# Moving one head pair's projection and convolution out of the delta stage into the seven-product stream, by way of DRAM

## The chip, the cores and the metric

One core of one Trainium2 chip runs the whole layer. The metric is the device time of one execution in microseconds (us). PE is TensorE, DVE is VectorE, ACT is ScalarE, POOL is GpSimd, SP is SyncE, whose queue issues most DMAs here.

## The reference, cut to what matters

The input is 1024 prompt rows and 64 rows of a running stream, 1088 rows of width 1024 in all. Branch B, the part that the change touches, has eight heads of 128; two heads make a *pair*, p = 0 to 3.

```python
y = einsum("bsd,de->bse", x, w_in)            # one projection, split into q, k, v, gates, ...
u = causal_conv(y[q|k|v of B], state_conv)    # width 4 along the rows, per channel, then SiLU
q, k = l2norm(q), l2norm(k)
per chunk of 64 rows:                         # 17 chunks: 16 of the prompt, 1 of the stream
    M     = strict_lower(beta * k k^T * decay)
    T     = inverse(I + M)
    v_new = T (beta v) - T (beta k decay) S   # S: state of the chunk before, 128x128 per head
    o     = q S decay + (q k^T * decay) v_new
    S     = S * decay + k^T v_new
Y_B = W_oB(rmsnorm(o) * silu(z_B))
x  <- LayerNorm(ALPHA * x + W_out(sig(g_A) * Y_A + sig(g_B) * Y_B))   # Y_A: window attention
```

## The kernel before, in words

Every fp32 product is made of three matmuls on rounded halves (hi·hi, hi·lo, lo·hi). The 1088 rows lie in SBUF as eight tiles `ring`, and weights come as tiles of 128 output channels (`wraw`, split into `whi`, `wlo`).

A weight tile is applied in one of two ways. **Direct** (`project`): three row groups of 384, 384 and 320 columns, 24 matmuls each, 72 matmuls and 26,112 columns for a tile. **Seven-product** (`stream`): two weight tiles together as a 2x2 block product with seven multiplications on quarter rows of 272 columns, 168 matmuls for both tiles; it needs sums of the input rows in SBUF (`ring2`), which are there only until attention ends.

The program runs in this order, in us of the profiled execution: loading, keys and values of branch A (0 to 117); `front`, a run of wide seven-product jobs for branch A's queries and its gate z (to 243); attention woven with narrow seven-product jobs of the merge gates (to 490); then branch B's delta stage (to about 1200), the two output projections, `out_b` and `final`.

The delta stage weaves two programs. The *chain* goes pair by pair: `ahead` (`logs`, `decay`, `products`, then `blocks`, a serial solve of 16x16 blocks on DVE), `steps` (17 delta steps, with `prep` a group of chunks ahead), `norm`. The *fill* is independent projection work: `pair_project` of the next pair (six tiles: q, k, v of two heads, each followed by the convolution on ACT and DVE into `plb`), a merge gate, `zb_project` of the pair before (two tiles), and at the end `out_a`. Each `yield` of the chain asks for so many fill columns before PE goes on with the chain: `PROD` behind each group of products, `BLOCKS[p]` behind the solve, the three of `STEP` behind the three parts of a step, `SHORT` in `prep` and `norm`. PE keeps this program order. The other engines are ordered by a scheduler: urgent work first, then chain, then fill. The chain of pair 0 can start when four of its six tiles are projected (`READY`).

The names in the rows: `pj` and `bg` are PSUM banks; `pre` and `acc` the convolution's input and running sum (L812: three taps for each row group, after a first tap on ACT); `gt` a gate or tanh buffer; L819 writes SiLU into `plb`; L833 the same for z_B. In `blocks`, `nF` (L891) comes just before the solve, L915 and L917 are its 15 rounds, `XC` (L921) its result; `prep` starts with `X` on POOL (L938) and PE's `X,MT`. In a step, `S,plb` is the product with the state, `R` L999, `R,U` the solve's product, `vn` L1009, `vn,t2k` the state update's product, `S` L1024.

Of the kernel before, what the change touches and what calls it, by code (L numbers as in the profile page):

```python
# [11 lines left out]
F32 = mybir.dt.float32  # L12
F32R = mybir.dt.float32r
# [9 lines left out]
SEQ = 1024  # L23
# [22 lines left out]
NORM = 11984  # L46
STEP = (2200, 2100, 1450)
PROD = 3672
# [7 lines left out]
class Build:  # L56
# [477 lines left out]
    def load_rope(self, pool, name):  # L534
        cs = self.t(pool, [128, 2, NT], "cs")
        self.nc.sync.dma_start(cs, self.I[name])
        self.cosT, self.sinT = cs[:, 0], cs[:, 1]
# [49 lines left out]
    def front(self):  # L587
# [3 lines left out]
        def query(j):  # L591
            held = {}

            def ev(m, a, ps, add):
                g, h = divmod(a // HN, 2)
                first = (m, g) not in held
                if first:
                    held[m, g] = self.t(self.rq, [128, 2, 2 * HN], "qsp", F32R, bufs=4)
                q = held[m, g]
# [18 lines left out]
            return ev  # L618

        def gate(dst, t, silu):  # L620
            def ev(m, a, ps, add):
                src = ps
                if add is not None:
                    src = self.t(self.gsp, [128, HN], "gs", bufs=5)
                    self.land(src, ps, add)
                th = self.t(self.gsp, [128, HN], "gs", bufs=5)
                with self.urgent():
                    nc.scalar.activation(th, src, AF.Tanh, scale=0.5)
                    if silu:
                        nc.vector.scalar_tensor_tensor(th, th, 1.0, src, ALU.add, ALU.mult)  # L630
                nc.sync.dma_start(dst[t + m, :, a : a + HN], th)
            return ev

        def jobs():
            yield True, query(0)
            yield True, gate(self.zA, 2, True)
            for j in range(1, 4):
                yield True, query(j)
            yield True, gate(self.zA, 4, True)
            yield True, gate(self.zA, 6, True)  # L640
            self.done = True
            for i in range(0, 16 - sum(GATES), 2):
                yield False, gate((self.gA, self.gB)[i // 8], i % 8, False)
# [137 lines left out]


    def pair_project(self, p, qkv):
        nc = self.nc
        self.order = LATER if p == 0 else EARLY
        for s in range(3):
            for h in range(2):
# [35 lines left out]

                yield from self.project(ev, edge=p + s + h == 0, w=None if p + s + h else self.first)
                self.ready[p] += 1

    def zb_project(self, p):
        nc = self.nc
        for h in range(2):
            def ev(g, a, n, ps):  # L830
                th = self.t(self.mp, [128, 384], "gt", bufs=4)
                nc.scalar.activation(th[:, :n], ps, AF.Tanh, scale=0.5)
                nc.vector.scalar_tensor_tensor(th[:, :n], th[:, :n], 1.0, ps, ALU.add, ALU.mult)  # L833
                nc.sync.dma_start(self.zsd[2 * p + h, :, a : a + n], th[:, :n])
            last = p == NPAIR - 1
            yield from self.project(ev, edge=last and h == 1, soon=last)

# [404 lines left out]
    def fills(self, qkv):  # L1242
# [3 lines left out]
        for p in range(NPAIR + 1):  # L1246
# [5 lines left out]
            if p > 0:  # L1252
                yield from self.gate_project([next(gates) for _ in range(GATES[p - 1])])
                yield from self.zb_project(p - 1)
            if p < NPAIR:
                yield from self.pair_project(p, qkv[p])
# [7 lines left out]
    def run(self):  # L1264
        tc = self.tc
        with ExitStack() as es:
# [10 lines left out]
            self.k_d = dp.tile([2, 64, 4, KW], F32, tag="k_d", name="k_d")  # L1277
            self.qd = dp.tile([2, 512, 2 * NT], F32, tag="q_d", name="q_d")
            self.hp = tc.cur_priority
            tc.cur_priority = self.hp + 1_000_000  # L1280
# [17 lines left out]
            with tc.tile_pool(name="mp", bufs=1) as self.mp:  # L1298
                with tc.tile_pool(name="plb", bufs=2) as self.plb:
                    with tc.tile_pool(name="bp", bufs=1) as self.bp:  # L1300
                        qkv, D = {}, [{} for _ in range(NPAIR)]
                        fill = self.fills(qkv)
                        next(fill)
                        before = iter(())
# [144 lines left out]
```

## Time and profile before

| | |
|---|---|
| three runs | 1408.94, 1410.66, 1410.67 us, median 1410.66 |
| the profiled execution | 1408.06 us, span 1406.3 us |
| busy | PE 97%, DVE 70%, ACT 44%, POOL 16% of the span |
| granted PE clock | 0.995 of full speed in the mean |
| DMA | 162.47 MB in 152,500 packets, 116 GB/s in the mean |

PE is busy nearly the whole span, so the time is the columns that PE streams plus the few places where it waits. How busy another engine is in the mean says little: it matters where PE waits for it.

### The profile page before, as it was taken

The numbers are of one execution on the slowest core, as the hardware profiler recorded it, in microseconds if no ns is written. First come the engines' busy times: TensorE is split into PE (matmuls) and PEld (weight loads), VectorE is DVE, ScalarE is ACT, GpSimd is POOL, SyncE is SP. The second block draws the span as 40 slices with busy tenths as digits, with TensorE's granted clock in tenths as the row PEclk, the third lists the DMA queues.
The fourth block names the chain that finished last, engine by engine and source line by source line (L and its number), as shares of the span: only waits on it lengthen the run. The fifth ranks groups of instructions, "written<-read, shape, count | busy, mean of one in ns | idle before, by whom it ended". The sixth has DMA issues, their size and how long they took to land. (4 is left out here: it accounts for less than half of the span.)

```text
span 1406.3 us, 30878 instructions
## 1 busy us (share of the span) xinstructions
PE 1364.9 (97%) x11850; PEld 1270.8 (90%) x11850; DVE 989.3 (70%) x2404; ACT 624.0 (44%) x1764; POOL 231.8 (16%) x379
## 2 busy tenths in 40 slices
PE   8889999999999999999999999999998999999997
PEld 7889999999989899988999889988998889999886
DVE  8668555877777568867796777867788555655675
ACT  5263444555555444356633665256642443422000
POOL 4323223111111023111221113021220100000000
PEclk9999999999999999999999999999999999999998
DMA  7425566666665420210321003210346225564221
GB/s 241 117 79 131 144 135 183 190 183 180 170 183 165 123 87 31 73 36 17 93 80 57 32 24 100 82 57 17 124 137 226 73 74 167 192 219 137 95 94 71
DMA packets 152500, 162.47 MB, mean 116 GB/s; under 512 B 54304, under 2 KB 135840, under 8 KB 151968
## 3 DMA queue, kind: packets, MB, share of 16 engines
q1 hardware_dynamic: 138368, 148.59, 35.4%
q10 hardware_dynamic: 13632, 10.78, 2.5%
q8 instruction: 94, 1.54, 0.5%
q0 software_dynamic: 352, 1.11, 0.2%
q14 instruction: 54, 0.44, 0.1%
HBM read 111.74 MB, written 48.70 MB: 114 GB/s over the span
## 5 line engine op out<-in xcount | busy, mean ns | idle before, releaser
L108 PE MATMUL pj<-ring,whi 128*128 128x384 f32 (+2 forms) x2856 | 678.3, 327 | 5.8 <-DVE gt L1134 4.0
L108 PEld LDWEIGHTS pj<-ring,whi 128*128 128x128 f32 x2856 | 480.1, 189 | 17.2 <-issue 13.3
L108 PE MATMUL pj<-ring,wlo 128*128 128x384 f32 (+2 forms) x1680 | 466.2, 321 | 0.9 <-DVE rsh L471 0.8
L108 PEld LDWEIGHTS pj<-ring,wlo 128*128 128x128 f32 x1680 | 288.4, 188 | 5.8 <-issue 4.1
L812 DVE SCALAR_TENSOR_TENSOR acc<-pre,sm,acc 128x384 f32<-128x384 f32 (+1 forms) x216 | 134.0, 627 | 24.2 <-ACT acc L810 20.7
L108 PE MATMUL pj<-ring,wx 128*128 128x272 f32 x756 | 109.7, 291 | 2.9 <-ACT u L365 2.8
L88 ACT ACTIVATE whi<-wraw 128x1024 fp32r<-128x1024 f32 (+2 forms) x72 | 66.7, 927 | 82.4 <-PE pj L108 48.8
L108 PEld LDWEIGHTS pj<-ring,wx 128*128 128x128 f32 x756 | 99.6, 188 | 3.8 <-ACT u L365 3.8
L91 DVE TENSOR_TENSOR wlo<-wraw,whi 128x1024 fp32r<-128x1024 f32 (+2 forms) x58 | 68.0, 1172 | 40.4 <-ACT whi L88 35.3
L108 PE MATMUL bg<-ring,whi 128*128 128x384 f32 (+2 forms) x408 | 84.5, 317 | 5.6 <-ACT ring L88 5.2
L108 PEld LDWEIGHTS bg<-ring,whi 128*128 128x128 f32 x408 | 65.6, 190 | 7.0 <-ACT ring L88 5.2
L108 PE MATMUL pj<-pl,ring 128*128 128x512 f32 (+1 forms) x240 | 70.1, 375 | 0.0
L704 ACT ACTIVATE P<-bg,nm 128x192 f32<-128x192 f32 (+2 forms) x136 | 54.4, 408 | 33.4 <-DVE nm L697 32.1
L1024 DVE SCALAR_TENSOR_TENSOR S<-S,dec,bg 128x128 f32<-128x128 f32 x128 | 38.7, 344 | 39.2 <-PE bg L108 38.3
L813 ACT ACTIVATE gt<-acc 128x384 f32<-128x384 f32 (+1 forms) x72 | 36.4, 505 | 62.3 <-DVE acc L812 62.0
L108 PE MATMUL bg<-ring,wlo 128*128 128x272 f32 (+2 forms) x288 | 63.5, 307 | 0.0
L1002 ACT ACTIVATE qs<-bg,egs 64x128 f32<-64x128 f32 x128 | 46.4, 362 | 29.1 <-DVE R L999 27.4
L999 DVE SCALAR_TENSOR_TENSOR R<-bg,negc,t2k 64x128 f32<-64x128 f32 x128 | 44.6, 348 | 16.1 <-PE bg L108 14.9
L336 POOL TENSOR_TENSOR sums<-wraw 128x512 f32<-128x512 f32 x14 | 18.3, 1308 | 220.4 <-DMA wraw<-w_tiles 109.4
L819 DVE SCALAR_TENSOR_TENSOR plb<-gt,acc 128x384 f32<-128x384 f32 (+1 forms) x96 | 43.1, 461 | 15.6 <-ACT gt L813 15.3
L108 PEld LDWEIGHTS pj<-pl,ring 128*128 128x128 f32 x240 | 44.1, 188 | 8.2
L810 ACT ACTIVATE acc<-pre,sm 128x384 f32<-128x384 f32 (+1 forms) x72 | 42.8, 597 | 15.6 <-DVE plb L819 5.9
(277 smaller groups left out, 2317.3 us busy)
## 6 DMA issues: line engine op xcount, KB each, us to landing
wraw<-w_tiles SPq DMA_DIRECT2D x80, 512.0 KB, 3.9
q_d<-qsp SPq DMA_DIRECT2D x32, 256.0 KB, 3.5
keys<-k_d SPq DMA_DIRECT2D x28, 256.0 KB, 4.2
q<-q_d SPq DMA_DIRECT2D x64, 96.0 KB, 2.7
gA_d<-gs SPq DMA_DIRECT2D x32, 136.0 KB, 2.2
plb<-prodA SPq DMA_DIRECT2D x8, 544.0 KB, 4.4
plb<-prodB SPq DMA_DIRECT2D x8, 544.0 KB, 5.1
z<-zA_d SPq DMA_DIRECT2D x16, 256.0 KB, 3.2
```

What stands on the lines that cost most here:

```text
L88: i = self.nc.scalar.activation(hi, raw, AF.Copy)
L91: self.nc.vector.tensor_tensor(lo, raw, hi.bitcast(F32), ALU.subtract)
L108: self.tc.keep_in_program_order(self.nc.tensor.matmul(o, l, r, start=start, stop=stop, skip_group_check=skip))
L336: sub = lambda d, x, y, op: nc.gpsimd.tensor_tensor(d, x, y, op)
L704: nc.scalar.activation(P[:, hf, k], ps[:, k], AF.Exp, bias=nm[:, hf, b : b + 1], scale=0.125, accum_out=sm[:, hf, b : b + 1])
L810: nc.scalar.activation(acc[:, :w], pre[:, 0:w], AF.Copy, scale=cw(0))
L812: nc.vector.scalar_tensor_tensor(acc[:, :w], pre[:, j : j + w], cw(j), acc[:, :w], ALU.mult, ALU.add)
L813: nc.scalar.activation(th[:, :w], acc[:, :w], AF.Tanh, scale=0.5)
L819: nc.vector.scalar_tensor_tensor(o, v(th), 1.0, v(acc), ALU.add, ALU.mult)
L999: nc.vector.scalar_tensor_tensor(R[HS[h]], ks[HS[h], col[h]], self.negc[HS[h], p, c : c + 1], e["vs"][HS[h], i], ALU.mult, ALU.add)
L1002: nc.scalar.activation(qs[HS[1 - h]], ks[HS[1 - h], col[h]], AF.Copy, scale=self.egs[HS[1 - h], p, c : c + 1])
L1024: nc.vector.scalar_tensor_tensor(Sn[:, h], S[:, h], self.egl[h][:, p, c : c + 1], kv[:, 0:128], ALU.mult, ALU.add)
```

## The change

The six tiles of pair 0 leave the delta stage's fill. They become three wide seven-product jobs `conv(0..2)` (q, k, v; both heads at once) in `front`, between the last query job and the last two z jobs. A job's evacuations land in one tile of whole rows (1024 prompt rows, three state columns, 64 stream rows). When all four quarters of a head are there, the convolution runs once over 1091 columns instead of three times over 384, 384 and 323, and the result goes to DRAM (`conv_d`). After attention, `pair_load` brings it into `plb` with six DMAs in runs of 64 elements, k and q at once, v later, and POOL makes the second copy of k.

Pair 0's z_B tiles, which were fill, are drained before the chain starts (144 matmuls), and `STEP` falls from (2200, 2100, 1450) to (1300, 1500, 1350). `BLOCKS`, `PROD`, `SHORT`, `NORM` stay.

```diff
-STEP = (2200, 2100, 1450)
+STEP = (1300, 1500, 1350)
...
+        def conv(s):
+            held, left, acc = {}, [4, 4], []
+
+            def ev(m, a, ps, add):
+                if m not in held:
+                    held[m] = self.t(self.rq, [128, 4 * HN + 8], "qsp", bufs=4)
+                pre = held[m]
+                n = min(HN, SEQ - a)
+                for d, c in ((3 + a, slice(0, n)), (1030, slice(n, HN)))[: 1 + (n < HN)]:
+                    c0, w = c.start, c.stop - c.start
+                    self.land(pre[:, d : d + w], ps[:, c], None if add is None else add[:, c])
+                left[m] -= 1
+                if left[m]:
+                    return
+                if not acc:
+                    acc.append(self.t(self.rq, [128, 2, NT + 4], "cs"))
+                ct, w = 8 * s + m, NT + 3
+                x, y = acc[0][:, m, :w], pre[:, :w]
+                nc.gpsimd.memset(pre[:, 0:3], 0.0)
+                nc.gpsimd.tensor_copy(pre[:, 1027:1030], self.sconv[:, ct, :])
+                nc.gpsimd.tensor_copy(self.ncv[:, ct, 0, :], pre[:, 1024:1027])
+                nc.gpsimd.tensor_copy(self.ncv[:, ct, 1, :], pre[:, 1091:1094])
+                cw = lambda j: self.convw[:, ct, j : j + 1]
+                nc.scalar.activation(x, y, AF.Copy, scale=cw(0))
+                for j in range(1, 4):
+                    nc.vector.scalar_tensor_tensor(x, pre[:, j : j + w], cw(j), x, ALU.mult, ALU.add)
+                nc.scalar.activation(y, x, AF.Tanh, scale=0.5)
+                nc.vector.scalar_tensor_tensor(y, y, 1.0, x, ALU.add, ALU.mult)
+                nc.sync.dma_start(self.conv_d[2 * s + m, :, :SEQ], pre[:, :SEQ])
+                nc.sync.dma_start(self.conv_d[2 * s + m, :, SEQ:], pre[:, 1027 : 1027 + DEC])
+            return ev
...
+            for s in range(3):
+                yield True, conv(s)
...
+    def pair_load(self, qkv):
+        nc = self.nc
+        rows = lambda s, h: self.conv_d[2 * s + h].rearrange("p (c t) -> p c t", t=CH)
+        with self.urgent():
+            for h in range(2):
+                nc.sync.dma_start(qkv[0][:, :, 4 + h], rows(1, h))
+                nc.sync.dma_start(qkv[0][:, :, 1 + h], rows(0, h))
+        for h in range(2):
+            nc.gpsimd.tensor_copy(qkv[0][:, :, 3 * h], qkv[0][:, :, 4 + h])
+        for h in range(2):
+            nc.sync.dma_start(qkv[1][:, :, h], rows(2, h))
+        self.ready[0] = 6
...
-        self.order = LATER if p == 0 else EARLY
...
-                yield from self.project(ev, edge=p + s + h == 0, w=None if p + s + h else self.first)
+                yield from self.project(ev)
...
-            last = p == NPAIR - 1
-            yield from self.project(ev, edge=last and h == 1, soon=last)
+            first, last = p + h == 0, p == NPAIR - 1
+            self.order = LATER if p == 0 else EARLY
+            yield from self.project(ev, edge=first or last and h == 1, w=self.first if first else None, soon=last)
...
+            if p == 0:
+                self.pair_load(qkv[0])
+            elif p < NPAIR:
                 yield from self.pair_project(p, qkv[p])
...
-                        next(fill)
+                        for _ in range(2 * 72):
+                            next(fill)
```

On **DVE**, inside pair 0's block solve (the rounds L915 and L917, in the changed program L964 and L966), before:

```order
L917 TENSOR_REDUCE t2k_7550<-t2k_7554 128x2x5
L915 TENSOR_TENSOR t2k_7554<-t2k_7550,t2k_7548 128x2x6x6
L819 SCALAR_TENSOR_TENSOR plb_6816<-gt_7720,acc_7719 128x4x64
L917 TENSOR_REDUCE t2k_7550<-t2k_7554 128x2x6
L819 SCALAR_TENSOR_TENSOR plb_6816<-gt_7720,acc_7719 128x64
L915 TENSOR_TENSOR t2k_7554<-t2k_7550,t2k_7548 128x2x7x7
L833 SCALAR_TENSOR_TENSOR gt_7760<-gt_7760,pj_7735 128x384
L917 TENSOR_REDUCE t2k_7550<-t2k_7554 128x2x7
```

and after, at the same rounds:

```order
L860 SCALAR_TENSOR_TENSOR acc_8233<-pre_8230,sm_220,acc_8233 128x384
L964 TENSOR_TENSOR t2k_8024<-t2k_8020,t2k_8018 128x2x8x8
L860 SCALAR_TENSOR_TENSOR acc_8233<-pre_8230,sm_220,acc_8233 128x384
L966 TENSOR_REDUCE t2k_8020<-t2k_8024 128x2x8
L860 SCALAR_TENSOR_TENSOR acc_8233<-pre_8230,sm_220,acc_8233 128x384
L964 TENSOR_TENSOR t2k_8024<-t2k_8020,t2k_8018 128x2x9x9
L966 TENSOR_REDUCE t2k_8020<-t2k_8024 128x2x9
L867 SCALAR_TENSOR_TENSOR plb_7585<-gt_8234,acc_8233 128x6x64
```

Convolution taps of pair 1 stand between the rounds where the end of pair 0's convolution and z_B work stood. Counted over the whole order (DVE instructions of the fill between the marks, before to after):

| pair | last product to `nF` | `nF` to `XC` | `XC` to the first `R` |
|---|---|---|---|
| 0 | 4 acc, 1 plb, 1 wlo: the same | acc 9 to 19, plb 6 to 9, gt 3 to 0 | acc 0 to 8, plb 1 to 4, gt 3 to 0 |
| 1 | 5 acc, 4 plb to 1 gt, 1 wlo | acc 0 to 19, plb 0 to 6, gt 2 to 0 | acc 6 to 11, plb 2 to 8, gt 4 to 0 |
| 2 | 1 acc, 3 plb to 1 gt | acc 0 to 9, plb 0 to 2, gt 4 to 2 | acc 0 to 6, plb 1 to 5, gt 2 to 0 |
| 3 | 5 acc, 4 plb, 2 gt to 1 plb | the same | gt 1 to 3, wlo 0 to 1 |

In the steps themselves, from the first to the last `R` of a pair, the order holds 30, 28, 30 and 0 acc before, and 18, 21, 22 and 0 after.

On **PE**, one delta step, before (`S,plb` opens the step, `R,U` follows `R`, `vn` rows close it; `pj` rows are fill):

```order
L108 MATMUL bg_8197<-S_8178,plb_6816 128x128 x2
L108 MATMUL bg_8206<-X_8040,MT_7309 32x32 x8
L108 MATMUL pj_8167<-ring_107,whi_8003 128x384
L108 MATMUL pj_8167<-ring_107,wlo_8004 128x384
L108 MATMUL pj_8167<-ring_108,whi_8003 128x384 x2
L108 MATMUL pj_8167<-ring_108,wlo_8004 128x384
L108 MATMUL pj_8167<-ring_109,whi_8003 128x384
L108 MATMUL bg_8225<-R_8200,U_7884 128x128
```

and after:

```order
L108 MATMUL bg_8720<-S_8689,plb_7576 128x128 x2
L108 MATMUL bg_8729<-X_8569,MT_7768 32x32 x8
L108 MATMUL pj_8716<-ring_106,whi_8533 128x384 x2
L108 MATMUL pj_8716<-ring_106,wlo_8534 128x384
L108 MATMUL bg_8745<-R_8723,U_8391 128x128
```

Of six fill matmuls between the state's product and `R,U` three are left here. In the mean over the steps the fill between them falls from 2091 to 1299 columns, between `R,U` and the `vn` products from 2221 to 1509, and between those and the next step from 1440 to 1339.

On **SP's queue**, after attention, the changed program issues this, where before only weight tiles and gate stores stood:

```order
L146 DMA wraw_7673<-w_tiles 128x1024
L823 DMA plb_7576<-conv_d 128x17x64
L824 DMA plb_7576<-conv_d 128x17x64
L823 DMA plb_7576<-conv_d 128x17x64
L824 DMA plb_7576<-conv_d 128x17x64
L882 DMA zs_d<-gt_7661 128x384
L882 DMA zs_d<-gt_7665 128x384
L882 DMA zs_d<-gt_7669 128x320
L146 DMA wraw_7777<-w_tiles 128x1024
```

Four loads of k and q stand ahead of the stores of z_B and of the next weight tile; the two of v stand a few rows later.

## Rows read from the trace of the kernel before

**Rows 1.** The page: the span, and each engine's busy time and instructions.

```profile
span 1406.3 us, 30878 instructions
PE 1364.9 (97%) x11850; PEld 1270.8 (90%) x11850; DVE 989.3 (70%) x2404; ACT 624.0 (44%) x1764; POOL 231.8 (16%) x379
```

**Rows 2.** Busy time by stretch: `front`, direct projection, pair 0's first `prep`, pair 0's steps.

```profile
core 0: us, PE busy (x) PEld busy (x) DVE busy (x) ACT busy (x) POOL busy (x), PEclk, DMA share, GB/s
165.00:240.00 75.00, 75.00 (x600) 75.00 (x599) 40.27 (x76) 32.80 (x74) 18.79 (x14) 1.00 0.72 175
505.00:540.00 35.00, 35.00 (x214) 35.00 (x213) 27.83 (x49) 19.41 (x41) 6.18 (x20) 1.00 0.14 46
593.00:604.00 11.00, 10.78 (x220) 9.35 (x221) 6.23 (x15) 4.58 (x16) 3.57 (x5) 1.00 0.30 100
604.00:683.00 79.00, 78.69 (x963) 68.64 (x962) 59.71 (x162) 49.19 (x160) 11.67 (x33) 1.00 0.09 27
```

**Rows 3.** PE's waits, whole span: total us, times, longest us.

```profile
PE bg L108 <- ACT vn L1009: 2.1, 6, 0.6
PE bg L108 <- POOL X L938: 1.7, 3, 0.7
PE bg L108 <- DVE R L999: 0.4, 1, 0.4
```

**Rows 4.** Busy time from `nF` to `XC`, pairs 0 to 3 (columns of rows 2).

```profile
565.20:592.40 27.20, 27.20 (x168) 27.17 (x167) 25.36 (x59) 9.06 (x18) 2.92 (x8) 1.00 0.18 60
726.20:747.50 21.30, 21.30 (x132) 21.30 (x131) 19.96 (x44) 5.76 (x10) 0.00 (x0) 1.00 0.20 70
888.70:911.30 22.60, 22.60 (x139) 22.54 (x138) 20.68 (x45) 5.87 (x10) 0.00 (x0) 1.00 0.26 89
1049.20:1084.60 35.40, 31.43 (x179) 30.96 (x177) 33.40 (x59) 14.35 (x17) 0.00 (x0) 0.95 0.67 222
```

**Rows 5.** PE's timeline at the first `X,MT` of pairs 0, 1 and 2.

```profile
593.22 0.45 PE L108 MATMUL bg<-X,MT 32*32 32x32 f32 x32 [0.47 <-POOL X L938]
...
758.05 0.45 PE L108 MATMUL bg<-X,MT 32*32 32x32 f32 x32
...
912.11 0.45 PE L108 MATMUL bg<-X,MT 32*32 32x32 f32 x32 [0.57 <-POOL X L938]
```

**Rows 6.** The page's costly groups and DVE's by form: busy us, mean ns | idle.

```profile
L812 DVE SCALAR_TENSOR_TENSOR acc<-pre,sm,acc 128x384 f32<-128x384 f32 (+1 forms) x216 | 134.0, 627 | 24.2 <-ACT acc L810 20.7
L819 DVE SCALAR_TENSOR_TENSOR plb<-gt,acc 128x384 f32<-128x384 f32 (+1 forms) x96 | 43.1, 461 | 15.6 <-ACT gt L813 15.3
L833 DVE SCALAR_TENSOR_TENSOR gt<-gt,pj 128x384 f32<-128x384 f32 (+1 forms) x21 | 10.8, 520 | 1.2 <-ACT gt L832 1.1
L91 DVE TENSOR_TENSOR qsp<-rraw,qsp 128x272 fp32r<-128x272 f32 x26 | 14.6, 561 | 6.9 <-ACT qsp L88 6.9
L91 DVE TENSOR_TENSOR wlo<-wraw,whi 128x1024 fp32r<-128x1024 f32 x52 | 64.9, 1249 | 36.5 <-ACT whi L88 31.5 <-PE bg L108 4.8
L893 DVE TENSOR_TENSOR MT<-MT,nF 128x1088 f32<-128x1088 f32 x4 | 5.2, 1291 | 0.1
```

**Rows 7.** One delta step of pair 0 in the timeline.

```profile
645.50 0.61 PE L108 MATMUL bg<-S,plb 128*128 128x128 f32 x4
...
646.49 0.71 DVE L999 SCALAR_TENSOR_TENSOR R<-bg,negc,t2k 64x128 f32<-64x128 f32 x2
648.09 0.38 PE L108 MATMUL bg<-R,U 128*128 128x128 f32 x2
648.51 0.37 ACT L1009 ACTIVATE vn<-bg,F 128x128 f32<-128x128 f32 x1 [0.48 <-PE bg L108]
649.46 0.45 PE L108 MATMUL bg<-vn,t2k 64*64 64x128 f32 x8
```

**Rows 8.** The page's DMA issues: KB each, median us to landing.

```profile
q_d<-qsp SPq DMA_DIRECT2D x32, 256.0 KB, 3.5
plb<-prodA SPq DMA_DIRECT2D x8, 544.0 KB, 4.4
```

More of the change, by code (lines that the diff above doesn't have):

```diff
@@ L534, in load_rope @@
     def load_rope(self, pool, name):
-        cs = self.t(pool, [128, 2, NT], "cs")
+        cs = self.t(pool, [128, 2, NT + 4], "cs")[:, :, :NT]
         self.nc.sync.dma_start(cs, self.I[name])
@@ L597, in ev @@
                 if first:
-                    held[m, g] = self.t(self.rq, [128, 2, 2 * HN], "qsp", F32R, bufs=4)
+                    held[m, g] = self.t(self.rq, [128, 4 * HN + 8], "qsp", F32R, bufs=4)[:, : 4 * HN].rearrange("p (s n) -> p s n", s=2)
                 q = held[m, g]
@@ L1254, in fills @@
                 yield from self.zb_project(p - 1)
-            if p < NPAIR:
+            if p == 0:
+                self.pair_load(qkv[0])
+            elif p < NPAIR:
                 yield from self.pair_project(p, qkv[p])
@@ L1278, in run @@
             self.qd = dp.tile([2, 512, 2 * NT], F32, tag="q_d", name="q_d")
+            self.conv_d = dp.tile([6, 128, NT], F32, tag="conv_d", name="conv_d")
             self.hp = tc.cur_priority
@@ L1396 @@
     qp = query_pairs()
-    cols = kc + zc[0:2] + qp[0] + zc[2:4] + qp[1] + qp[2] + qp[3] + zc[4:8]
+    conv = lambda p: [2560 + 1024 * s + 128 * (2 * p + h) + ar for s in range(3) for h in range(2)]
+    cols = kc + zc[0:2] + qp[0] + zc[2:4] + qp[1] + qp[2] + qp[3] + conv(0) + zc[4:8]
     gates = iter([6672 + 128 * t + ar for t in range(16)])
@@ L1400 @@
     for p in range(NPAIR):
-        for s in range(3):
-            cols += [2560 + 1024 * s + 128 * (2 * p + h) + ar for h in range(2)]
+        cols += conv(p) if p else []
         cols += [next(gates) for _ in range(GATES[p])]
```

## Prediction

> **What bounds the kernel now.** I read the page first: PE is busy 1364.9 of 1406.3 us [rows 1], and DVE, the next engine, 989.3. So the time is PE's columns plus PE's waits, and a change is worth the columns that it saves less the waits that it opens. Then I read two stretches for the price of a column [rows 2]. In `front`, PE runs 600 matmuls of 272 columns in 75.00 us, 0.125 us each; in the direct projection it runs 214 in 35.00 us, 0.1636 us each, at 26,112 / 72 = 363 columns, so 0.451 us for 1000 columns. Both are without a gap at full clock.
>
> Third, the waits. In the whole span the delta stage's own links make PE wait very little: 2.1 us for `vn`, 1.7 us for `X` behind the block solves, 0.4 us for `R` [rows 3]. But look at how near those waits are. Between `nF` and `XC`, DVE is busy 25.36 of 27.20 us for pair 0, 19.96 of 21.30, 20.68 of 22.60, and 33.40 of 35.40 for pair 3 [rows 4]: in these four windows DVE is the bound, not PE, and the fill's columns only just cover it. PE reaches the first `X,MT` and waits 0.47 us for pair 0 and 0.57 us for pair 2; for pair 1 it comes at 758.05 without a wait, 10.5 us behind the end of the `XC` window, of which `X` itself takes 0.8 (592.40 to 593.22 in pair 0): 9.7 us of slack [rows 4, 5]. So of a microsecond of DVE work added there, pairs 0 and 2 pay nearly all.
>
> **The change part by part.**
>
> *Columns.* Six direct tiles go: 6 x 72 = 432 matmuls at 0.1636 us, 70.7 us. Three wide jobs come: 3 x 168 = 504 at 0.125 us, 63.0 us. That is -7.7 us, if nothing waits on either side. The two z_B tiles only move.
>
> *Convolution in `front`.* A job takes PE 168 x 0.125 = 21.0 us. DVE is busy 40.27 of 75.00 us there, 11.3 us a job [rows 2]. A conv job adds eight passes over 1091 columns. The trace has no such tap; the nearest row is L893 with 1088 columns, 1.291 us, so 10.3 us a job; by three of today's taps (3 x 0.627) it would be 15.0 us [rows 6]. The query job's rounding, eight subtractions of 0.561 us or 4.5 of the 11.3 [rows 6], isn't in it. DVE thus comes to 17 to 22 us of 21. PE waits only at the bound's upper end, some 1 us a job: 0 to +3, and I take +0.5, near the first row, whose width it has.
>
> *The loads.* Four loads of 544 KB must land before the first products. Loads of 544 KB into the same tile took 4.4 us [rows 8]; one behind the other they take 4 x 4.4 = 18 us. In runs of 256 bytes the nearest row is `q_d<-qsp`, 256 KB in 3.5 us; by size a load would be 7.4 us, and four 30 us. The cover is the drained z_B, 144 x 0.1636 = 23.6 us, and two `PROD` of 3672 columns, 3.3 us: 27 us. So 0 by the first price and +3 by the second, up to +5 if the tile comes free late. I take 0, since the first row has the same tile and size. SP's queue has the z_B stores behind them, and weight tiles behind those; they would be late only where the four are. The v loads are needed a whole block solve later. POOL's two copies of k are covered by the same solve, since the first step needs them only then.
>
> The Trainium skill, "DMA: Bandwidth & Descriptors", section Specifications, says that a transfer wants at least 512 bytes for line rate and that below it the engine reads, modifies and writes. The 256-byte `q_d` row shows no collapse: 256 KB in 3.5 us against 544 KB in 4.4 us. By the page the loads would be the rival with the late load below; by the row they are hidden.
>
> *The block solves.* This is the large term. Before, the fill under pair 0's solve was the tail of its own tiles and z_B; now it is pair 1's convolution, the heaviest fill for DVE. Prices are 0.627 us for a tap, 0.461 for an L819, 0.520 for an L833, 1.249 for a `wlo` [rows 6].
> Pair 0: ten taps, three L819 more, three L833 fewer between `nF` and `XC`: 6.27 + 1.38 - 1.56 = +6.1 us. The window's idle of 1.84 us can take in a part; PE already waits 0.47. So +4.3 to +6.1; I take +4.5, and 0 is the lower end if DVE lets the taps fall behind the rounds.
> Pair 1: 19 taps, six L819 more, two L833 fewer: 11.9 + 2.8 - 1.0 = +13.7. Ahead of `nF`, five taps and four L819 go and one L833 and one `wlo` come: -3.2. The slack is 9.7, and the window's idle 1.34. Net 13.7 - 3.2 - 9.7 = +0.8 less that idle: I take 0, between 0 and +2.
> Pair 2: nine taps, two L819 more, two L833 fewer: +5.5; ahead of `nF` -1.5; idle 1.92 takes some: +2 to +4, I take +2.5.
> Pair 3: nothing between, 5.5 us of work less ahead of `nF`: its wait at `X` (0.7, the longest of the three) goes, -0.6.
> Sum +6.4.
>
> *The first `prep`.* From `XC` to the first step PE has 11.0 us, busy 10.78, DVE 6.23 [rows 2]. The chain here is short PE products with ACT, POOL and DVE between, each covered by `SHORT`, 2310 columns or 1.04 us. DVE gets eight taps and three L819 more, three L833 fewer in pair 0 (+4.8), and +3 or so in the others. Two of DVE's answers (kd, vs) can then be late by a tap or an L819 each. Bounds 0.5 and 4.5 us over four pairs; I take +2, half a microsecond a pair.
>
> *The steps.* In one step of pair 0, `R` ends at 647.20 and `R,U` starts at 648.09 [rows 7]: slack 0.89. `vn` ends at 648.88 and its products start at 649.46: slack 0.58. The fill is cut by 792, 712 and 101 columns, 0.36, 0.32 and 0.05 us. Slacks of 0.53 and 0.26 us are left, so the chain itself still fits. But one tap in front of `R` or `S` costs it 0.63 us, and that fitted before and no longer does: 0.1 to 0.37 us of wait each time. There are 61 taps in the steps now (88 before); where half of them meet the chain, 30 x 0.1 to 0.37 gives 3 to 11 us. DVE is busy 59.71 of 79.00 us in pair 0's steps [rows 2]; with a stretch shorter by about 17 x 0.72 = 12 us and 12 taps less it is 52 of 67, the same share, which speaks against a gain too. Pair 3 has no taps. I take +4, ends +2 and +10.
>
> **The sum.** 1408.06 - 7.7 + 6.4 + 2 + 4 + 0.5 + 0 = 1413.3 us for an execution like the profiled one. The median of the runs lies 2.6 above it (1410.66), so I say **1416 us**. Within 0.2%, 2.8 us, of 1410.66 nothing can be told from no change.
>
> **The rivals.**
>
> *Slower by DVE (the forecast), 0.50.* Its own range is 1413.5 to 1424: the steps at +10 and the solves at their upper ends give 1424.
>
> *The cover holds: faster, 0.29.* DVE's rounds are narrow, and a scheduler that knows the chain is urgent could put taps into the round trips to ACT and leave the rounds where they are; the steps have 27 taps fewer, so they could even shed their 2.5 us of waits. Then the columns come through: 1410.66 - 7.7 = 1403, up to 1407 with half of the +6.4 and a little of the rest. For it speaks that PE waited only 0.47 and 0.57 us with the present taps in these windows; against it, that DVE was at 93% and 92% in them. It decides below +4.9 us of waits in all.
>
> *It cancels, 0.21.* The waits come to 5 to 10.5 us, and the time lies within 1408 to 1413.5. The pair 0 and 2 solves alone, +7, would do that.
>
> *A late load, in the forecast's chance with 0.06.* The 256-byte runs take 7.4 us each and start only when attention's tiles are free; PE stands before the first products for 5 us or more, with the steps as forecast: about 1420 to 1424. It decides where four loads take over 27 us from the end of the stream.
>
> *`front` doesn't save.* If a tap over 1091 columns costs 1.88 us or more, DVE is over 21 us a job, the last z jobs start late, and 3 us of the 7.7 are gone there. It adds to any of the cases, and I give it 0.15 within them.
>
> The range takes in a part of the faster case and the whole of the forecast: 1404 to 1424, with 0.09 left out below and 0.09 above. Chances: faster 0.29, same 0.21, slower 0.50.
>
> **What the changed profile would show.** 504 more matmuls of 272 columns at 0.125 us in `front`, which ends 63 us later, with DVE at 80% or more there. No wait before pair 0's first products behind `plb<-conv_d`. A wait on `X` behind the solve of 4 to 5 us for pair 0, 2 to 3 us for pair 2, none for pair 3; windows from `nF` to `XC` of about 32 us for pair 0 and 35 for pair 1. `R`, `vn` and `S` together 4 us or more above today's 2.5 in PE's waits. The prediction is wrong if `X` arrives within a microsecond of PE in pairs 0 and 2, since more than half of the loss hangs on it; or if the step waits stay under 4 us, which would mean that the scheduler holds the taps behind the chain.

## The result and the profile after

The changed kernel takes 1443.34 us in the median (1442.39 to 1444.72, 4 runs), the kernel before 1409.80 us in the runs beside it: a ratio of 1.0239, 95% interval 1.0221 to 1.0257. It is 33.5 us slower. The forecast said slower, but 1416 us, and its range ended at 1424.

The page of the changed kernel, span and engines (to be laid beside [rows 1]):

```profile
span 1440.6 us, 31077 instructions
PE 1372.5 (95%) x11922; PEld 1270.7 (88%) x11922; DVE 996.0 (69%) x2389; ACT 623.8 (43%) x1747; POOL 254.7 (18%) x381
```

The span grew by 34.3 us. PE's idle time, span less busy, went from 41.4 to 68.1 us: +26.7. Its busy time grew by 7.6 us, although the columns should have made it 7.7 us less. Most of that difference is the clock: the granted mean fell from 0.995 to 0.986 of full speed, and 0.014 x 1440.6 = 20.2 us lost against 0.005 x 1406.3 = 7.0 us is some 13 us. That is an upper bound, since the mean also counts time in which PE stands idle. In the stretches granted 0.50 PE works 28.3 us, against 6.8 before; by an estimate that takes half of that time as lost, the clock costs 10.7 us more than before. So: idle +26.7, clock +10.7, columns -7.7, and 4.6 us that I can't put down to one of them.

PE's waits in the changed kernel that the text uses, whole span (engine, line, what it waited for: total us, times, longest), to be laid beside [rows 3]:

```profile
PE pj L108 <- DVE gs L413: 6.7, 2, 6.3
PE bg L108 <- POOL X L987: 6.4, 2, 3.5
PE bg L108 <- ACT vn L1058: 5.4, 11, 1.0
PE pj L108 <- ACT pre L851: 4.7, 1, 4.7
PE bg L108 <- DVE R L1048: 4.4, 11, 1.0
PE bg L108 <- DMA q<-q_d: 3.0, 1, 3.0
PE bg L108 <- ACT Y L1011: 2.3, 1, 2.3
PE pj L108 <- DVE gt L1183: 1.4, 1, 1.4
```

`X`, `vn` and `R` are the links that the forecast named, and they are late. But the first and the sixth row are new, and all but 0.4 us of them lies in attention, where the forecast had expected nothing. The fourth is new too, and lies in the delta stage.

**Where the time went, by place.** From the start to pair 0's first product the trace of before has 544.9 us and that of after 600.8: +55.9. By columns it should be 63.0 - 4 x 11.78 + 2 x 11.78 = +39.4 (three jobs come, four direct tiles go, two z_B tiles come). So 16.5 us are lost ahead of the delta stage. From there to the end of the span it is 861.4 us before and 839.8 after, -21.6, where four tiles less of fill should make it -47.1: 25.5 us are lost from the delta stage on.

**The solves.** Busy time in the windows from `nF` to `XC` of pairs 0 to 2, pair 0's steps, and the stretch of conv jobs, in the changed kernel (us, then busy of PE, PEld, DVE, ACT, POOL, PE clock, DMA share, GB/s; the first three answer to [rows 4], the last two to [rows 2]):

```profile
620.20:650.50 30.30, 28.33 (x173) 28.03 (x171) 29.66 (x69) 14.39 (x29) 4.25 (x16) 1.00 0.11 36
773.20:803.00 29.80, 29.80 (x184) 29.80 (x182) 29.15 (x67) 12.88 (x26) 5.32 (x16) 1.00 0.15 51
931.20:956.90 25.70, 22.97 (x142) 22.61 (x140) 24.65 (x55) 9.04 (x17) 2.26 (x7) 1.00 0.17 56
662.20:733.00 70.80, 67.15 (x886) 56.04 (x886) 49.87 (x147) 41.86 (x144) 11.58 (x25) 1.00 0.08 26
220.00:282.00 62.00, 62.00 (x496) 62.00 (x496) 49.36 (x61) 30.88 (x55) 27.04 (x33) 1.00 0.31 98
```

The solve windows are longer by 3.1, 8.5 and 3.1 us, and DVE has 10, 23 and 10 instructions more in them. In the conv jobs PE loses nothing: 496 matmuls in 62.00 us are 0.125 us each, with DVE at 80%.

**The wait for `pre`.** At pair 3's products PE waits 4.7 us for a bank that ACT hasn't emptied. ACT's copy out of it (`pre`) stands in ACT's order behind `norm` of pair 2 (L1155), and that waits 5.7 us until a store to `prodB` has landed:

```profile
1060.82 0.40 ACT L1155 ACTIVATE t2k<-plb,ro 128x128 f32<-128x128 f32 x1 [5.73 <-DMA prodB<-t2k]
...
1062.52 0.90 PE L108 MATMUL pj<-ring,whi 128*128 128x320 f32 x2 [4.67 <-ACT pre L851]
```

Before, ACT had the same kind of wait (4.4 us, until 1023.0), but PE had no need to wait for it.

**The clock.** The same columns for stretches right behind PE's waits for `gs`, pair 0's `X` and pair 2's `X` in the changed kernel (the second row is pair 0's wait itself):

```profile
345.10:352.00 6.90, 6.90 (x39) 6.90 (x39) 2.20 (x6) 1.69 (x6) 0.00 (x0) 0.66 0.57 171
648.30:651.10 2.80, 0.23 (x2) 0.00 (x0) 2.50 (x6) 2.66 (x5) 0.46 (x2) 1.00 0.00 0
651.10:655.00 3.90, 3.64 (x113) 3.37 (x114) 3.84 (x10) 2.08 (x6) 1.64 (x4) 1.00 0.02 4
957.40:964.20 6.80, 6.49 (x112) 5.77 (x112) 4.94 (x11) 1.34 (x4) 2.06 (x4) 0.50 0.01 2
```

Behind the wait of 3.5 us for pair 2's `X`, PE works 6.5 us at 0.50, which is 1.2 of 2.4 GHz, and loses about half of that; behind that of 6.3 us it has 0.66 in the mean of 6.9 us. Behind pair 0's wait of 2.8 us the clock stays at 1.00. A wait can thus cost about its own length again, but it doesn't always.

**The late loads of q.** The changed kernel's SP queue around the start of attention (start us, us, queue, line, operation):

```profile
288.18 0.43 SPq L650 DMA_DIRECT2D conv_d<-qsp  x1
295.65 0.32 SPq L664 DMA_DIRECT2D zA_d<-gs  x1
...
309.05 0.54 SPq L583 DMA_DIRECT2D keys<-k_d  x1
309.64 3.88 SPq L720 DMA_DIRECT2D q<-q_d  x8
...
339.55 2.01 SPq L720 DMA_DIRECT2D q<-q_d  x4
341.61 1.89 SPq L664 DMA_DIRECT2D zA_d<-gs  x4
```

and the first row of what the queue waited for between 285 and 346 us:

```profile
SPq L664 <- DVE gs L413: 12.8, 5, 7.3
```

DVE in the longest of these waits, between the stores at 288 and 295 us (start us, us, line, operation):

```profile
289.42 2.38 DVE L646 SCALAR_TENSOR_TENSOR cs<-qsp,sm,cs 128x1091 f32<-128x1091 f32 x1
...
292.31 1.34 DVE L646 SCALAR_TENSOR_TENSOR cs<-qsp,sm,cs 128x1091 f32<-128x1091 f32 x1
293.58 0.43 DVE L413 TENSOR_TENSOR gs<-pj,u 128x272 f32<-128x272 f32 x1
```

SP issues in order. Its z stores wait for DVE's `gs`, which stands behind conv's taps over whole rows (L646) in DVE's order; the loads of q wait behind the stores. The first goes out at 309.64, as soon as the load of keys ahead of it is issued (309.59), so nothing held it but the queue; and PE starts the scores at 313.90. Before, the first load went out at 228.9 for scores at 243.1. Then it turns round: the last four z stores stand behind q loads, go out at 341.61, and PE waits 6.3 us for a `gs` buffer.

### The profile page after: what moved, and what is told of

Its sections match the earlier page's. It is cut to its first block, busy times and chain, and to the rows that moved or that the text cites. A ratio compares the mean times of both kernels' runs of the same rounds, so it can differ in the third digit from the quotient of the medians.

```text
span 1440.6 us, 31077 instructions
## 1 busy us (share of the span) xinstructions
PE 1372.5 (95%) x11922; PEld 1270.7 (88%) x11922; DVE 996.0 (69%) x2389; ACT 623.8 (43%) x1747; POOL 254.7 (18%) x381
## 5 line engine op out<-in xcount | busy, mean ns | idle before, releaser
L108 PE MATMUL pj<-ring,whi 128*128 128x384 f32 (+2 forms) x2640 | 621.7, 327 | 8.6 <-ACT pre L851 4.7
L108 PEld LDWEIGHTS pj<-ring,whi 128*128 128x128 f32 x2640 | 441.7, 190 | 20.3 <-issue 8.9
L108 PE MATMUL pj<-ring,wlo 128*128 128x384 f32 (+2 forms) x1608 | 431.0, 320 | 1.9 <-DVE rsh L471 0.8
L108 PEld LDWEIGHTS pj<-ring,wlo 128*128 128x128 f32 x1608 | 272.0, 189 | 7.4 <-issue 4.3
L108 PE MATMUL pj<-ring,wx 128*128 128x272 f32 x864 | 127.5, 295 | 12.8 <-DVE gs L413 6.7
L108 PEld LDWEIGHTS pj<-ring,wx 128*128 128x128 f32 x864 | 116.2, 192 | 14.1 <-DVE gs L413 7.1
L860 DVE SCALAR_TENSOR_TENSOR acc<-pre,sm,acc 128x384 f32<-128x384 f32 (+1 forms) x162 | 98.1, 610 | 12.7 <-ACT acc L858 10.3
L108 PE MATMUL bg<-ring,whi 128*128 128x272 f32 (+2 forms) x480 | 94.7, 312 | 5.1 <-ACT ring L88 4.4
L1048 DVE SCALAR_TENSOR_TENSOR R<-bg,negc,t2k 64x128 f32<-64x128 f32 x128 | 44.6, 349 | 16.4 <-PE bg L108 14.5
L108 PEld LDWEIGHTS bg<-ring,wlo 128*128 128x128 f32 x360 | 54.3, 189 | 0.3 <-DVE wlo L91 0.2
L108 PE MATMUL bg<-ring,wx 128*128 128x272 f32 x360 | 50.3, 288 | 0.2 <-DVE gs L413 0.2
```

The source lines that it names most:

```text
L108: self.tc.keep_in_program_order(self.nc.tensor.matmul(o, l, r, start=start, stop=stop, skip_group_check=skip))
L860: nc.vector.scalar_tensor_tensor(acc[:, :w], pre[:, j : j + w], cw(j), acc[:, :w], ALU.mult, ALU.add)
L1048: nc.vector.scalar_tensor_tensor(R[HS[h]], ks[HS[h], col[h]], self.negc[HS[h], p, c : c + 1], e["vs"][HS[h], i], ALU.mult, ALU.add)
```

## Experiments

**1 and 2. Conv's place in `front`, and its passes.** Two kernels made from the changed one. In the first the conv jobs come earlier (the weight tiles follow); the second leaves out the convolution of pair 0, not its projections.

```diff
...
             yield True, gate(self.zA, 2, True)
+            for s in range(3):
+                yield True, conv(s)
             for j in range(1, 4):
                 yield True, query(j)
-            for s in range(3):
-                yield True, conv(s)
...
```
```diff
...
-                nc.scalar.activation(x, y, AF.Copy, scale=cw(0))
-                for j in range(1, 4):
-                    nc.vector.scalar_tensor_tensor(x, pre[:, j : j + w], cw(j), x, ALU.mult, ALU.add)
-                nc.scalar.activation(y, x, AF.Tanh, scale=0.5)
-                nc.vector.scalar_tensor_tensor(y, y, 1.0, x, ALU.add, ALU.mult)
...
```

> The changed kernel with the three conv jobs moved ahead of the last three query jobs; all else as in the change. Theory A: attention starts late and then loses its stores, because conv was the last user of the tiles whose SBUF attention's q tiles take over, so the first q loads went out 4 us before they were needed (14 us before the change) and the last z stores got behind q loads on SP's queue. Then the waits of 3.0 us for q and 6.3 us for gs go, with the half-speed stretches behind them, and the time falls by 10 to 17 us, to 1426 to 1433. Rival B: what delays the front is DVE's whole-row passes as such; they are all still there, only earlier, so the time stays within 4 us of 1443.

> The changed kernel with pair 0's convolution left out in front (no taps, no tanh, no SiLU on ACT and DVE; raw projections are stored), so that its output isn't the reference's. By theory A (late release of tiles and the order on SP's queue) most of the loss goes as well, since the tiles come free earlier: 10 to 17 us less, 1426 to 1433. By rival B (DVE's passes delay the front) the same or more. Together with the run that moves the jobs: both fall by A, only this one by B. Neither changes the delta stage, so at least 15 us above the kernel before stay.

Moved ahead: 1429.62 us (ratio to before 1.0134, 1.0115 to 1.0153), 13.7 us less than the change. Without the passes: 1426.34 us (1.0121, 1.0106 to 1.0136), 17.0 us less. With the jobs moved, the first q load goes out at 295.95 for scores at 310.53, and the waits for `q` and the 6.3 us for `gs` are gone. From the start to pair 0's first product it is 590.1 and 586.3 us, where the change has 600.8: of the 16.5 us lost there, 10.7 and 14.5 come back. From there to the end of the span they take 838.9 and 840.4 us, where the change has 839.8. Both runs fall, as theory A had it. But what A named, tiles that come free late, is not what the rows show: the first load of q waited for nothing of its own when the queue came to it, and the queue's rows name `gs` on DVE. DVE's passes are the delay (so far B is right), and most of it is lost because they stand just ahead of attention's loads.

**3. STEP alone.**

```diff
 # the kernel before
-STEP = (2200, 2100, 1450)
+STEP = (1300, 1500, 1350)
```

> The kernel before with STEP alone set to (1300, 1500, 1350); all projections as before, so the columns of the whole program are the same and fill that the steps no longer take is done later. If the thinner cover by itself makes the steps wait: R, vn and their like rise from 2.5 us to some 10, and with lower clock behind the waits the time is 8 to 15 us above before (1418 to 1425). Rival: the steps wait only because other fill (pair 2's and 3's taps) meets them; then the time stays within 4 us of 1410.

1413.94 us, ratio 1.0029 (1.0017 to 1.004), 4.0 us above before. PE's waits in the stage:

```profile
PE bg L108 <- ACT vn L1009: 6.8, 13, 1.2
PE bg L108 <- DVE R L999: 4.1, 9, 1.1
PE pj L108 <- DVE gt L1134: 2.4, 1, 2.4
PE bg L108 <- POOL X L938: 0.5, 1, 0.5
```

With STEP alone changed the steps wait 10.9 us instead of 2.5, as the theory had it. The time doesn't decide between the two: it rises by half of what the theory expected, and 1413.94 lies just within the 4 us of 1410 that the rival allowed. (A smaller STEP also shifts which fill meets which link, so this run isn't the cover's thickness and nothing else.) Where the rest went: the wait for `gt` is 1.6 us shorter and those for `X` are 1.2, and no stretch of the steps runs at a lower clock.

**4. The stage's schedule alone.** The kernel before, with all of pair 0's tiles and its z_B drained ahead of the chain, as direct projections, and the new STEP: the delta stage's order of the change without conv jobs, loads or fewer columns.

```diff
 # the kernel before
-STEP = (2200, 2100, 1450)
+STEP = (1300, 1500, 1350)
...
-                        next(fill)
+                        for _ in range(8 * 72):
+                            next(fill)
```

> The kernel before with the delta stage's schedule of the change and nothing else of it: all six tiles of pair 0 and both its z_B tiles are projected directly and drained before the chain, and STEP is (1300, 1500, 1350). No seven-product conv, no loads, and the same columns as before; pair 0's chain now meets pair 1's tiles as its first fill. Theory: most of the loss is the stage's, because the fill that is left meets the block solves with its taps and the steps have less cover; from pair 0's first products to the end the changed kernel lost 26 us against its columns, so the time is 20 to 28 us above before, 1430 to 1438, with waits for X of 2 to 4 us in pairs 0 and 2. Rival: the stage waits because of what comes with the loads or with the front; then the time is that of the run with STEP alone, 1411 to 1418.

1434.88 us, ratio 1.018 (1.0163 to 1.0197): 25.5 us above before. The page's engines and PE's longest waits in its delta stage:

```profile
PE 1375.1 (96%) x11850; PEld 1274.7 (89%) x11850; DVE 985.1 (69%) x2404; ACT 626.3 (44%) x1764; POOL 233.9 (16%) x379
```
```profile
PE bg L108 <- POOL X L938: 6.4, 2, 3.5
PE bg L108 <- ACT vn L1009: 5.4, 11, 1.0
PE pj L108 <- ACT pre L803: 4.6, 1, 4.6
PE bg L108 <- DVE R L999: 4.3, 11, 1.0
PE bg L108 <- ACT Y L962: 2.3, 1, 2.3
```

These are the changed kernel's rows of the stage, to a tenth of a microsecond, without conv jobs and without loads. The stage's loss comes from STEP, from which fill is left when the chain starts, and from how it meets the chain. Since STEP alone costs 4 us, some 21 us come with the shift of the fill, if the two simply add up.

**5. Light tiles under pair 0's solve.** The changed kernel, with two tiles of pair 1 drained first, a third woven with the products, and pair 0's z_B under the solve.

```diff
...
+            elif p == 1:
+                work = self.pair_project(1, qkv[1])
+                yield from itertools.islice(work, 3 * 72)
+                yield from self.zb_project(0)
+                yield from work
...
```

> The changed kernel with its fill in another order: two tiles of pair 1 are drained before the chain, a third is woven with pair 0's products, and pair 0's two z_B tiles, which ask little of DVE, come under pair 0's block solve. If heavy taps under the solve cause the wait for X there: 2.8 us in the changed kernel goes to 0.5 or less, and with the lower clock around it some 4 us of the time, to about 1439; pair 2's wait of 3.5 us stays or falls by half. Rival: the solve waits for its own ACT and POOL round trips; then the wait stays at 2.8 us and the time at 1443.

1447.96 us (1.0275, 1.0259 to 1.0291), 4.6 above the change. The solve did what was expected: its window is 21.8 us instead of 30.3, and `X` has 5.3 us to spare. But `Y`, two links on, is 2.0 us late, and in the drained stretch PE waits 5.6 us for `pre`: ACT's copy stands behind a weight split and then waits until the last gate store (`gB_d`) has landed, and both the weight tile and that store lie behind the loads on SP's queue. The time says nothing on the question, the window does.

**6, 7 and 8. More cover.** Three kernels made from that of experiment 1, in which only one of pair 0's z_B tiles is drained. The freed columns go under the solves, into the steps, or, with two gate tiles brought back as direct fill, into both.

```diff
-                        for _ in range(2 * 72):
+                        for _ in range(72):
 # 6
+BLOCKS = (76000, 76000, 62000, 79000)
+STEP = (1400, 1558, 1350)
 # 7
+STEP = (1600, 1600, 1358)
 # 8
+BLOCKS = (76000, 76000, 62000, 79000)
+STEP = (1800, 1850, 1450)
+GATES = (0, 1, 2, 1)
```

> The run with the conv jobs moved ahead (1429.6 us), and now only one of pair 0's two z_B tiles is drained before the chain; its 26,112 columns serve as cover: 6000 more under pair 0's and pair 1's block solve (that is pair 1's 76000 kept, pair 0's raised to it), 10,000 more under pair 2's, and the rest in STEP (1400, 1558, 1350). No column is added or left out. Theory: the delta stage lacks cover where the serial solve waits; then X's waits of 2.9 and 3.5 us fall below 0.6 each, with the half-speed stretch behind pair 2's, and the time falls by 6 to 11 us, to 1419 to 1424. Rival: the drained tile was what hid the loads from DRAM; then PE waits before pair 0's first products for some of the 11.8 us, and the time stays within 3 us of 1430.

> As the run before, but the undrained tile goes to the steps alone: STEP (1600, 1600, 1358), BLOCKS as in the change. If thin cover makes the steps wait, their idle time (about 11 us over the four pairs) falls by a third to a half, the X waits stay at 2.9 and 3.5 us, and the time falls by 3 to 6 us, to 1424 to 1427. If the taps alone make the waits, nothing changes beyond 2 us.

> As the run with more cover under the solves, and two of the merge gate's tiles leave the seven-product stream and become direct fill in the delta stage again (one under pair 2's chain, one at the end), with STEP (1800, 1850, 1450). That adds 144 x 0.1636 - 168 x 0.125 = 2.6 us of columns and gives 52,224 columns of cover that ask DVE for nothing. Theory: the stage's serial chain and not the columns sets the time, so the step waits fall to some 4 us and the time by 3 to 8 us below the run with solve cover alone, to 1412 to 1419. Rival: cover is no longer short; then the time rises by 2.6 us.

1438.84 us (1.0216, 1.02 to 1.0232), 1431.73 us (1.0159, 1.0144 to 1.0174) and 1445.79 us (1.0261, 1.024 to 1.0281), where the base has 1429.62: all three missed, and on the wrong side, though the second by 2.1 us only, which the intervals don't tell from the base. PE's longest waits in the delta stage of the first, and the issue and the wait on which the third row hangs:

```profile
PE bg L108 <- ACT Y L1011: 9.0, 3, 3.9
PE bg L108 <- ACT vn L1058: 8.7, 17, 1.3
PE bg L108 <- POOL w1k L894: 6.5, 1, 6.5
...
573.14 0.42 SPq L664 DMA_DIRECT2D gB_d<-gs  x1
...
578.63 0.61 POOL L894 TENSOR_TENSOR w1k<-cf,ghi 128x256 fp32r<-128x256 f32 x1 [7.07 <-DMA gB_d<-gs]
```

The waits for `X` of pairs 0 and 2 did go; `Y` waits in their place, 9.0 us in three places. Columns of convolution fill bring their own taps, so more of that cover brings more work for DVE and ACT, and the next link is late: in pair 0 ACT's copy of `Y` stands behind a tanh that waited 1.6 us for DVE's taps, and behind a weight split. And the undrained tile was cover for what the loads hold up: POOL's first `w1k` of the chain waits until attention's last gate store, `gB_d`, has landed, and that store stands on SP's queue behind the four loads and three stores of z_B. (POOL's copies of k were done at 571.6, 7 us earlier.) Of 11.8 us of cover taken away, 6.5 us came back as a wait, so the change had 5.3 us to spare there. In the second, the steps' wait (`vn` and `R`) fell only from 9.8 to 8.0 us. The third measures the gates' return along with all that; its steps idle less, but attention, without them, has 4.5 us more idle time than in experiment 1.

**9 and 10. The same fill in another order.** From the kernel of experiment 1; BLOCKS, STEP and what is drained stay. z_B tiles and gates, which have no taps, are put where the solves fall. The second differs from the first only in pair 3.

```diff
 # 9
...
+            elif p == 1:
+                work = self.pair_project(1, qkv[1])
+                yield from itertools.islice(work, 72)
+                yield from self.zb_project(1)
+                yield from work
+            elif p < NPAIR:
+                late = self.zb_project(p)
+                yield from itertools.islice(late, 144 if p == 2 else 72)
+                yield from self.gate_project([next(gates)])
+                yield from self.pair_project(p, qkv[p])
+                yield from late
...
 # 10, pair 3
...
+                yield from self.zb_project(p)
+                work = self.pair_project(p, qkv[p])
+                yield from itertools.islice(work, 5 * 72)
+                yield from self.gate_project([next(gates)])
+                yield from work
...
```

> The run with the conv jobs moved ahead (1429.6 us) with the same tiles of fill in another order, BLOCKS, STEP and the drained tiles unchanged: pair 1's z_B stands behind pair 1's first tile, so under pair 0's solve; pair 2's z_B and a gate ahead of pair 2's tiles, under pair 1's solve; one z_B tile of pair 3 and a gate ahead of pair 3's tiles, under pair 2's solve. Theory: what counts is which fill meets the solves, not how much; with tiles that have no taps there the windows from nF to XC shrink from 30, 30 and 26 us to 21 to 25, the waits for X and Y (2.9, 2.4, 3.5 us) go, and with the clock behind them the time falls by 6 to 12 us, to 1418 to 1424. Rival: the taps that are displaced meet the steps instead, whose waits grow by as much; then the time stays within 4 us of 1430.

> The run with the reordered fill (1428.9 us), with one more shift at its end: both z_B tiles of pair 3 ahead of pair 3's tiles and the gate just ahead of the last of them, so that no store of z_B stands behind the loads of prodB on SP's queue while PE waits for its buffer. Theory: that wait (9.0 us, and before the change 4.0 us at the same place) was all that hid the gain of the reordered fill; it goes, and the time falls by 7 to 11 us, to 1418 to 1422. Rival: the last tile's stores or ACT's copies wait there in its place; then the time stays within 3 us of 1429.

The first: 1428.85 us (1.0135, 1.012 to 1.015). Its windows from `nF` to `XC`, pairs 0 to 2:

```profile
608.00:629.90 21.90, 21.90 (x135) 21.90 (x135) 19.57 (x45) 4.51 (x8) 0.00 (x0) 1.00 0.21 68
758.80:780.00 21.20, 21.20 (x131) 21.20 (x130) 18.76 (x43) 4.29 (x8) 0.00 (x0) 1.00 0.25 83
920.90:941.50 20.60, 20.60 (x129) 20.57 (x128) 19.25 (x41) 5.11 (x8) 0.00 (x0) 1.00 0.19 63
```

and PE's longest waits in its delta stage, with DVE's rows ahead of the end of the first:

```profile
PE pj L108 <- DVE gt L881: 9.0, 1, 9.0
PE bg L108 <- DVE R L1048: 5.4, 13, 1.0
PE bg L108 <- ACT vn L1058: 5.2, 12, 0.8
...
1071.18 9.69 DVE L91 TENSOR_TENSOR ring<-plb,ring 128x1088 fp32r<-128x1088 f32 x8
...
1082.29 0.47 DVE L881 SCALAR_TENSOR_TENSOR gt<-gt,pj 128x320 f32<-128x320 f32 x1
```

The windows are 22, 21 and 21 us instead of 30, 30 and 26, and no wait for `X` or `Y` is left. The steps hardly pay for it, 10.6 instead of 9.8 us. What eats the gain is one wait of 9.0 us in pair 3's solve, for the bank that DVE reads into `gt` (L881): eight passes that split `prodA`'s rows into `ring` for `out_a`, 9.7 us in a row, and a weight split stand ahead of it on DVE. With that tile moved, the second takes 1421.82 us (1.0085, 1.0068 to 1.0102): 7.8 us less than the kernel of experiment 1, 21.5 less than the change. The time came as expected, but not by the cause that was named: the store of z_B went out (1082.79) only when `gt` was there, so its place on SP's queue can't have held PE up. And the rival came true in part: the same eight passes on ACT (8.1 us in a row) stand ahead of a copy of `pre` now, and PE waits 5.8 us for that, and 2.7 us for pair 2's `X`.

**11. Gates as fill, in that order.** As 10, with two gate tiles more in the delta stage (GATES = (0, 2, 2, 0)) and STEP = (1650, 1850, 1450).

> The run before this one, and two gate tiles leave the seven-product stream for the delta stage's fill (+2.6 us of columns), one more ahead of pair 2's and one ahead of pair 3's tiles, with STEP raised by what they hold to (1650, 1850, 1450). Theory: with light tiles under the solves and thicker cover in the steps, whose waits are 11 us now, the steps wait 4 to 7 us; the time is that of the run before less 0 to 5 us, 1414 to 1421. If cover in the steps is worth nothing, it is 2 to 4 us more than that run.

1427.63 us (1.0131, 1.0116 to 1.0146), 5.8 above 10: outside what was expected. The steps' waits fell from 10.5 to 5.9 us, as the theory wanted, but attention, without that job, has 4.1 us more idle time, and the direct tiles cost 2.6 us of columns; some 3.7 us of the 5.8 I can't place. Gates are worth more where they were.

No version tried beats the kernel before.

## Why the prediction was wrong, point by point

The direction was right, and the waits that the forecast named did come: 14.3 us for `X`, `Y` and the steps, where it had 12.4. But they are only a third of the 42 us that the changed kernel loses against its columns. The size was off by 27 us: some 13 in `front`, and some 13 in the delta stage, where a wait and the clock were not in the sum. The runs separate the two places.

*Columns, -7.7.* Right: 72 matmuls more (504 come, 432 go) and 0.125 us each.

*Convolution in `front`, +0.5.* This is the step that failed. Its price was right: a tap took 1.35 us in the median against 1.29, DVE was at 80%, PE lost nothing in the jobs. But it asked only whether DVE keeps up with PE, not who else waits for DVE there. SP's z stores do, attention's q loads stand behind them, and then stores behind loads. Up to pair 0's first product 16.5 us were lost instead, and 13.7 us of the time go when the jobs stand elsewhere. The prediction looked at DVE's share and never at SP's queue there, whose stores and loads conv was put in front of. Its rival that `front` doesn't save had the right place with the wrong condition: it asked for a tap of 1.88 us.

*Loads, 0.* Right in effect, by luck. The page of the changed kernel has 7.3 us for a load of 544 KB, the upper price, not the 4.4 that I took:

```profile
plb<-conv_d SPq DMA_DIRECT2D x6, 544.0 KB, 7.3
plb<-prodB SPq DMA_DIRECT2D x8, 544.0 KB, 5.5
```

One behind the other, as the prediction had them, four would have taken 29 us of the 27. They overlapped: issued from 573.4 on, the last had landed by 586.6, 14 us before the first product. What came nearest to being late was the gate store behind them on SP's queue, with some 5 us to spare (experiment 6). The Trainium skill, "DMA: Bandwidth & Descriptors", section Specifications, asks for 512 bytes or more for line rate; this row agrees with it, 7.3 us in 256-byte runs against 4.4 for as much from `prodA` [rows 8], and I had set the rule aside on a row of half the size. How much of that is the run length isn't shown: loads in long runs from `prodB` took 5.5 us, and no run changed the run length alone.

*Block solves, +6.4.* Near. The waits for `X` went from 1.7 to 6.4 us, +4.7: pair 0 +2.4 (said 4.5), pair 2 +3.0 (2.5), pair 1 none (0), pair 3's gone (-0.6). Pair 1's window grew by 8.5 us, to 29.8 where 35 had been said, and used up 7.4 us of its slack where the sum had 10.5; pair 0's is 30.3, said 32. So the added taps cost less there than their price.

*First `prep`, +2.* +2.3, all in pair 1, for `Y`.

*Steps, +4.* `vn` and `R` went from 2.5 to 9.8 us: +7.3, inside its bounds of 2 and 10. By itself STEP is worth 4 us of time (experiment 3).

*Not in the sum: `pre`.* 4.7 us, at pair 3's products. It comes in experiment 4 as well (4.6 us), so it belongs to the stage's schedule. On the other side PE's wait for `gt` in pair 3 shrank from 4.0 to 1.4 us.

*Not in the sum at all: the clock.* I took each wait at its length. Behind several of them PE worked at half speed, which cost 10.7 us more over the span than before, and a row that I had quoted showed it: pair 3's solve before, with a wait in it, at 0.95 [rows 4]. In experiment 4, with the same matmul count as before, idle time grew by 16.5 us and busy time by 10.2; the clock accounts for 12.9 - 7.0 = 5.9 of these, and 4 us of busy time I can't place.

The pieces, taken from different runs, add up: the stage's schedule alone +25.5 (experiment 4), conv's place +13.7 (experiment 1), columns -7.7 make +31.5 of the 33.5 us. What the rival of the held cover got wrong is now plain: the fill that went out was not spare. Four tiles less of it left the chain with convolution tiles under the solves of pairs 0 to 2, where z_B and gate tiles had stood (under pair 0's also the end of its own), and the order alone can give back some 8 us of that (experiment 10).

## What to carry to other kernels

Work that covers a serial chain is not free to take away: a cheaper way to do it elsewhere gains its columns and loses the cover, and what is left may meet the chain at its worst place; look which tile lies under which link, not how many columns there are. When work with a heavy tail on one engine is moved, list everyone who waits for that engine at the new place, in-order DMA queues first. And price a wait of a few microseconds at up to twice its length where the rows show the clock falling behind such waits.

## What the runs showed of the hardware

The granted clock after a wait isn't a function of the wait's length alone: behind 3.5 us it was 0.50, behind 2.8 us it stayed 1.00, and behind a wait of 2.3 us for pair 1's `Y` the stretch from 810 to 814 us had 0.58. In experiment 4 the same wait of 2.8 us for pair 0's `X` was followed by 0.64 (second row). I don't know what decides it; the runs don't separate it.

```profile
810.00:814.00 4.00, 3.85 (x78) 3.38 (x80) 3.80 (x9) 1.00 (x3) 1.37 (x2) 0.58 0.44 135
643.50:648.00 4.50, 4.47 (x110) 4.04 (x111) 3.99 (x11) 1.97 (x5) 1.96 (x4) 0.64 0.01 4
```

And six of the 24 passes of 1091 columns took 2.4 us instead of 1.3. In each of the six an addition of weights on POOL was already under way when the pass began, as here at the tap of 289.42 above (POOL's timeline of the changed kernel); the tap of 292.31, with POOL idle, took 1.34. Two passes began before such an addition did, at 238.23 and 260.20 against 238.92 and 260.98, and took 1.35. Copies of three columns on POOL beside a tap did not slow it. The change makes more of such meetings, since it gives `front` 24 long passes and three more jobs' sums; what they cost no run took apart.

```profile
288.91 1.73 POOL L336 TENSOR_TENSOR wraw<-wraw,sums 128x512 f32<-128x512 f32 x1
```
